# A decoder trunk on one core: where the tiles start in SBUF

## The chip, the cores and the metric

The kernel runs on one core of a Trainium2 chip. The metric is device time in microseconds (us), the median over several executions of one kernel; smaller is better. A profile is one execution, taken by the hardware profiler. PE (TensorE) multiplies matrices; a matmul has a stationary operand, which a weight load (PEld) puts into the array, and a moving operand that streams past it. DVE (VectorE) and ACT (ScalarE) do elementwise work, POOL (GpSimd) some of it, and SP (SyncE) issues all DMAs. All operands of PE come out of SBUF, which has 128 partitions; a tile of [128, 512] float32 takes 2,048 bytes in each partition, and its address is the byte at which it starts in every partition.

## What is computed

A sequence of 2,048 rows of width 1,024 goes through one retention layer and one sliding-window attention layer:

```
x = x + (rms(retention(q, k, v)) * silu(gate)) @ a_w_out      # 4 heads, chunks of 128
k, v = shared_kv(x)                                           # 2 key/value heads of 64
x = x + (swa(q, k, v, bias, sinks) * silu(gate)) @ b_w_out    # 16 heads, window of 128
```

with q, k, v and gate from an rms-normalised x times an input weight, a causal decay in the retention, and an attention over the block's own 128 keys and the 128 before, with a bias by distance and a sink in the softmax.

## The kernel before

**Precision.** Every large product is made of three matmuls in float32r: an operand `t` is split into `hi` (a rounded copy that ACT writes) and `lo = t - hi` (DVE, in the second layer partly POOL), and PE adds hi*hi, hi*lo and lo*hi into the same PSUM bank. `wload` (L104 to L124) does this with a weight tile: a DMA into a buffer with the tag "raw" (three buffers), the cast into "whi", the subtraction into "wlo". A matmul of this kind has a moving operand of [128, 512] and a stationary one of [128, 128]. In the rows a PE instruction is written as result<-moving,stationary.

**The retention layer (phase A).** 16 units, one for each of four row groups of 512 and four heads. `main` makes q and k (`project_qk`, L483 to L485, moving `xhi`/`xlo`, stationary `whi`/`wlo`), then v and gate: in the first four units with `proj` (L147 to L149, moving the weights, stationary x), in the other twelve with seven products of a Strassen scheme (`strassen`, L365 to L367), four of which take sums of x (`xhi_S`, `xlo_S`) as stationary operand. `ret` does the chunks of the retention: scores (L563), transposes of k (L583), the state's change (L604 to L606, moving `vhi`/`vlo`, stationary `khi`/`klo`), the output (L612 to L614, moving `Shi`/`Slo`, stationary `qhi`/`qlo`; L615 to L617, moving v, stationary `shi`/`slo`), transposes of the gated output (L640). `out_a` multiplies by the output weight (`pp_ao`, L143 to L145, moving `ohi_r`/`olo_r`, stationary `whi`/`wlo`).

**The attention layer (phase B).** 8 units: keys and values once for each group, q (L147 to L149), gates (L143 to L145, moving `xhi`), scores (L867), transposes of the probabilities (L888), the output (L904), the output projection (`pp_bo`, the same lines L143 to L145, moving `ohi_t`/`olo_t`).

**Order.** A scheduler interleaves the units; the program's order on each engine is fixed at build time.

**Where the tiles lie.** Pools lie one behind the other in SBUF in the order in which they are opened, and within a pool tiles lie in the order in which their tags first appear, each rounded up to 32 bytes: `const`, `xtp` (x hi and lo), `wp` (raw, whi, wlo), `small`, then the pools of phase A (`av` v, `ca` constants, `a1` most working tiles, `a2`, `ag` gate, `as` sums, `ax` the residual), which phase B's pools (`cb`, `b1`, `b2`) replace. Small tiles that come in between move all tiles behind them. In the built program, the starting bytes modulo 512 are:

| tiles | before | after the change |
|---|---|---|
| `ident`, `ident_r` | 128 | 0 |
| `ones` | 192 | 0 |
| `xhi`, `xlo`, raw, `whi`, `wlo` (all phases) | 320 | 0 |
| `vhi`, `vlo` | 192 | 0 |
| phase A: q, k, `ohi_r`, `olo_r`, `Shi`, `Slo`, `qhi`, `qlo`, `khi`, `klo`, `shi`, `slo`, gate, `xhi_S`, `xlo_S`, S, `x1` | 288 | 0 |
| phase B: `bias`, `kst`, `qs`, `qst`, `ohi_t`, `olo_t`, P, `pTs`, `vst`, `res`, gate | 320 | 0 |
| `rb` of `small` (read by DVE and POOL alone) | 320 | 128 |

A slice that PE reads starts a multiple of 512 bytes into its tile (`vst` and half of `qs` a multiple of 256), so the table holds for the operands too.

The functions that the change touches:

Of the kernel before, what the change touches and what calls it, by code (L numbers as in the profile page):

```python
# [12 lines left out]
F32 = mybir.dt.float32  # L13
F32R = mybir.dt.float32r
BF16 = mybir.dt.bfloat16
AF = mybir.ActivationFunctionType
# [3 lines left out]
P = 128  # L20
D = 1024
KT = D // P
T = 512
MT = T // P
RH = 4
DK = 256
DV = 512
HD = 64
QH = 16
KVH = 2  # L30
GQ = QH // KVH
EPS = 1e-6
NBUCK = 32
# [4 lines left out]
RAW = 3  # L38
# [20 lines left out]
def tile_yoco(ctx, tc, x, x_t, w_qk, w_vg, wo_a, w_kv, w_b, wo_b, ag, kvg, bg, kng, qng,  # L59
              relb, sinks, cos_t, sin_t, mask_t, vdec, epsd, onehot, out):  # L60
    nc = tc.nc
# [5 lines left out]
    const = ctx.enter_context(tc.tile_pool(name="const", bufs=1))  # L67
    xtp = ctx.enter_context(tc.tile_pool(name="xtp", bufs=1))
    wp = ctx.enter_context(tc.tile_pool(name="wp", bufs=3))
    small = ctx.enter_context(tc.tile_pool(name="small", bufs=4))  # L70
# [2 lines left out]
    xmid = [dram.tile([KT // 2, P, 2, T], F32, name=f"xmid{i}") for i in range(NG)]  # L73
    sqs = [dram.tile([P, T], F32, name=f"sqs{i}") for i in range(NG)]

    ident = const.tile([P, P], F32, name="ident")
    make_identity(nc, ident)
    ident_r = const.tile([P, P], F32R, name="ident_r")
    nc.vector.tensor_copy(ident_r, ident)
    neghalf = const.tile([P, GQ], F32, name="neghalf")  # L80
    nc.vector.memset(neghalf, -0.5)

    warm = const.tile([P, 1], F32, name="warm")
    nc.scalar.activation(warm, neghalf[:, :1], AF.Silu)

    ones = const.tile([P, P], F32, name="ones")
    nc.vector.memset(ones, 1.0)
    kvgs = const.tile([P, KT], F32, name="kvgs")
    bgs = const.tile([P, KT], F32, name="bgs")
    psum = {}  # L90

    def pbank(tag, name):
        return pp.tile([P, 512], F32, tag=tag, name=name)
# [104 lines left out]
    def bias_rows():  # L198


        oh = wp.tile([NBUCK + 1, 384], F32, tag="raw", bufs=RAW, name="oh")
        nc.sync.dma_start(oh, onehot)
        rb = const.tile([NBUCK + 1, QH], F32, name="rb")
        nc.vector.memset(rb, 1.0)
        nc.sync.dma_start(rb[:NBUCK, :], relb)
        bp = pbank("a", "biasp")
        nc.tensor.matmul(bp[:QH, :384], rb, oh, start=True, stop=True)
        bsb = wp.tile([QH, 384], F32, tag="raw", bufs=RAW, name="bsb")
        nc.vector.tensor_copy(bsb, bp[:QH, :384])
        nc.sync.dma_start(bd, bsb)  # L210
        yield
        for h in range(QH):
            nc.sync.dma_start(bdr[h], bd[h].partition_broadcast(P))
            yield
# [4 lines left out]
    def phase_a(pa):  # L219
        cst = pa["const"]  # L220
        p1, p2, vp, gp, xsp = pa["p1"], pa["p2"], pa["v"], pa["g"], pa["xs"]
        H = T // 2
        ags = cst.tile([P, KT], F32, name="ags")
        nc.sync.dma_start(ags, ag)
        mask = cst.tile([P, P], F32, name="mask")
        vd = cst.tile([P, RH], F32, name="vd")
        ep = cst.tile([P, RH], F32, name="ep")
        S_d = [dram.tile([P, 2, DV], F32, name=f"Sd{h}") for h in range(RH)]
        units = [(g, h) for g in range(NG) for h in range(RH)]
        nu = len(units)  # L230
# [310 lines left out]
        def ret(u):  # L541
            g, h = units[u]
            n = f"r{u}"
# [48 lines left out]
            for c in range(MT):  # L592
# [36 lines left out]
                        if c < MT - 1:  # L629
                            split_state(S32, d, parts)  # L630

                junk = small.tile([P, DV], BF16, tag="junk", bufs=1, name=f"jo_{n}_{c}")
                ss = small.tile([P, 1], F32, tag="ss1", name=f"sso_{n}_{c}")
                nc.scalar.activation(junk, op, AF.Square, accum_out=ss)  # L634
                r = rsqrt_mean(ss, DV, 1, f"o_{n}_{c}", eps=es[c])
# [67 lines left out]
        for _ in main(0):  # L703
            pass
        bias = bias_rows()
        for u in range(nu - 1):

            g, h = units[u + 1]
            if u + 1 in (1, 3, 4, 5):
                behind.append(stage_sums({1: 0, 3: 1, 4: 2, 5: 3}[u + 1]))  # L710
            if h == 2 and g + 1 < NG:
                behind.append(row_stats(g + 1))
                behind.append(stage_rows(g + 1))
            drive(tc, main(u + 1), ret(u), 2 if u + 1 < PLAIN else 3, 0)
            for _ in itertools.islice(bias, 2 if u >= RH else 0):
                pass
            if u < nu - 2:
                for _ in out_a(u):
                    pass
        pre = prep_b0()  # L720
        drive(tc, itertools.chain(out_a(nu - 2), itertools.islice(pre, 2)), ret(nu - 1), 1.5, 0)
        for _ in itertools.chain(out_a(nu - 1), pre):
            pass


    def phase_b(pb):
        cst = pb["const"]
        p1, p2 = pb["p1"], pb["p2"]
        gq = cst.tile([P, HD], F32, name="gq")
        gk = cst.tile([P, HD], F32, name="gk")  # L730
        nc.sync.dma_start(gq, qng.partition_broadcast(P))
# [1 line left out]
        nc.vector.scalar_tensor_tensor(gk, gk, HD ** -0.5, gq, op0=ALU.mult, op1=ALU.mult)  # L733
        snk = cst.tile([P, QH], F32, name="snk")
        nc.sync.dma_start(snk, sinks.partition_broadcast(P))
        nsnk = cst.tile([P, QH], F32, name="nsnk")
        nc.vector.tensor_scalar_mul(nsnk, snk, -1.0)
        bias = cst.tile([P, QH, 2 * P], F32, name="bias")
        nc.sync.dma_start(bias, bass.AP(tensor=bdr.tensor, offset=bdr.offset + P - 1,
                                        ap=[[383, P], [P * 384, QH], [1, 2 * P]]))  # L740

        units = [(g, kv) for g in range(NG) for kv in range(KVH)]
        nu = len(units)
        st = {"xt": first["xt"]}

        kst = cst.tile([P, KVH * 2, 2 * MT + 1, P], F32R, name="kst")

        def main(u):
            g, kv = units[u]
# [243 lines left out]
    with ExitStack() as es:  # L993
        mk = lambda name, bufs: es.enter_context(tc.tile_pool(name=name, bufs=bufs))
        psum["phase"] = "b"
        psum["pool"] = es.enter_context(tc.tile_pool(name="psb", bufs=1, space=bass.MemoryType.PSUM))
        phase_b(dict(const=mk("cb", 1), p1=mk("b1", 1), p2=mk("b2", 2)))
# [92 lines left out]
```

## Time and profile before

| | us |
|---|---|
| median of 3 runs (lowest, highest) | 2535.78 (2533.89, 2538.88) |
| the profiled execution: time | 2535.8 |
| the profiled execution: span from first to last instruction | 2534.0 |
| PE busy | 2469.2 (97%) |
| DVE busy | 1718.3 (68%) |
| ACT busy | 1128.5 (45%) |
| POOL busy | 476.7 (19%) |

How to read it: the busy time of PE counts a matmul from its start to its modelled end, and the matmuls overlap each other. A busy PE is therefore not a PE at its peak; how fast it really goes is read from the starts of matmuls that follow each other.

### The profile page before, as it was taken

The numbers are of one execution on the slowest core, as the hardware profiler recorded it, in microseconds if no ns is written. First come the engines' busy times: TensorE is split into PE (matmuls) and PEld (weight loads), VectorE is DVE, ScalarE is ACT, GpSimd is POOL, SyncE is SP. The second block draws the span as 40 slices with busy tenths as digits, with TensorE's granted clock in tenths as the row PEclk, the third lists the DMA queues.
The fourth block names the chain that finished last, engine by engine and source line by source line (L and its number), as shares of the span: only waits on it lengthen the run. The fifth ranks groups of instructions, "written<-read, shape, count | busy, mean of one in ns | idle before, by whom it ended". The sixth has DMA issues, their size and how long they took to land.

```text
span 2534.0 us, 32377 instructions
## 1 busy us (share of the span) xinstructions
PE 2469.2 (97%) x11816; PEld 1996.7 (79%) x11816; DVE 1718.3 (68%) x2953; ACT 1128.5 (45%) x2008; POOL 476.7 (19%) x393
## 2 busy tenths in 40 slices
PE   8999999999999999999999999999899999999998
PEld 6888787888888888888888888777677777777886
DVE  5546675785867667668666576677867677667766
ACT  4333233544435435436345344335544455444553
POOL 0000000110000020000020000042335444353360
PEclk9999999999999999999999999999899999999999
DMA  8434873576735445455354243364233342342432
GB/s 293 140 108 140 270 258 114 197 274 214 240 104 189 150 159 166 157 204 183 122 200 148 85 157 112 101 247 161 76 117 121 108 151 77 127 146 80 133 114 95
DMA packets 141035, 395.05 MB, mean 156 GB/s; under 512 B 16411, under 2 KB 28876, under 8 KB 140876
## 3 DMA queue, kind: packets, MB, share of 16 engines
q1 hardware_dynamic: 140876, 392.99, 46.7%
q8 instruction: 93, 1.52, 0.2%
q14 instruction: 66, 0.54, 0.1%
HBM read 321.60 MB, written 74.47 MB: 156 GB/s over the span
## 4 chain that ended last, share of the span: by engine, by line
PE 79%; DMA 9%; DVE 8%; ACT 2%; issue 1%; POOL 0%; SPq 0%; DVEq 0%; ACTq 0%
PE pp_ao L145 4%; PE pp_ao L143 4%; PE pp_ao L144 4%; PE o_t L904 2%; PE s_t L867 2%; PE pT_t L888 2%; PE pp_bo L143 1%; PE pp_bo L144 1%; PE pp_bo L145 1%; DMA res<-xmid 1%; DVE xlo_b L186 1%; PE o_r L613 1%; PE ot_r L640 1%; PE o_r L614 1%; PE o_r L612 1%
## 5 line engine op out<-in xcount | busy, mean ns | idle before, releaser
L143 PE MATMUL pp_ao<-ohi_r,whi_ao 128*128 128x512 f32 x512 | 201.6, 398 | 4.1 <-DVE x_r L676 2.1
L144 PE MATMUL pp_ao<-olo_r,whi_ao 128*128 128x512 f32 x512 | 203.7, 398 | 0.0
L101 POOL TENSOR_SCALAR r_o_r<-sso_r,ep 128x1 f32<-128x1 f32 x48 | 28.7, 597 | 920.8 <-ACT jo_r L634 920.8
L878 ACT ACTIVATE P_t<-P_t,nm_t 128x256 f32<-128x256 f32 (+1 forms) x256 | 127.7, 499 | 162.8 <-DVE nm_t L870 162.2
L145 PE MATMUL pp_ao<-ohi_r,wlo_ao 128*128 128x512 f32 x512 | 198.7, 398 | 0.1
L870 DVE CUSTOM_DVE_ANT_0 P_t<-s_t,bias,nsnk 128x256 f32<-128x256 f32 (+1 forms) x256 | 116.4, 470 | 38.7 <-PE s_t L867 37.8
L121 ACT CAST whi_ao<-raw_ao 128x1024 fp32r<-128x1024 f32 x64 | 67.1, 1048 | 155.5 <-issue 54.4
L123 DVE TENSOR_TENSOR wlo_ao<-raw_ao,whi_ao 128x1024 fp32r<-128x1024 f32 x64 | 78.2, 1223 | 83.9 <-ACT whi_ao L121 83.8
L700 ACT CAST Shi_r<-S 128x512 fp32r<-128x512 f32 x120 | 69.9, 617 | 114.8 <-PE o_r L614 89.8
L143 PEld LDWEIGHTS pp_ao<-ohi_r,whi_ao 128*128 128x128 f32 x512 | 96.1, 188 | 28.0 <-DVE x_r L676 2.5
L145 PEld LDWEIGHTS pp_ao<-ohi_r,wlo_ao 128*128 128x128 f32 x512 | 96.6, 189 | 24.6 <-DVE wlo_ao L123 1.2
L144 PEld LDWEIGHTS pp_ao<-olo_r,whi_ao 128*128 128x128 f32 x512 | 96.8, 189 | 23.2 <-issue 0.2
L867 PE MATMUL s_t<-kst,qst_b 128*128 128x256 f32 (+1 forms) x512 | 103.8, 300 | 9.2 <-DVE nm_t L870 9.0
L701 DVE TENSOR_TENSOR Slo_r<-S,Shi_r 128x512 fp32r<-128x512 f32 x120 | 85.3, 736 | 37.8 <-ACT Shi_r L700 37.8
L867 PEld LDWEIGHTS s_t<-kst,qst_b 128*128 128x128 f32 x512 | 84.9, 193 | 30.7 <-DVE nm_t L870 12.1
L627 DVE SCALAR_TENSOR_TENSOR S<-S,dl_r 128x512 f32<-128x512 f32 x112 | 74.6, 681 | 43.1 <-PE dl_r L606 42.9
L884 DVE TENSOR_SCALAR P_t<-P_t,den_t 128x256 f32<-128x256 f32 (+1 forms) x256 | 96.9, 441 | 1.8
L676 DVE TENSOR_TENSOR x_r<-x_r,pp_ao 128x512 f32<-128x512 f32 x128 | 84.4, 683 | 17.9 <-PE pp_ao L145 17.2
L143 PE MATMUL pp_bo<-ohi_t,whi_bo 128*128 128x512 f32 x224 | 89.4, 408 | 1.2 <-DVE gate_b L831 1.1
L144 PE MATMUL pp_bo<-olo_t,whi_bo 128*128 128x512 f32 x224 | 89.5, 399 | 0.0
L123 POOL TENSOR_TENSOR wlo_bo<-raw_bo,whi_bo 128x1024 fp32r<-128x1024 f32 x28 | 71.1, 2541 | 93.4 <-ACT whi_bo L121 87.0
L145 PE MATMUL pp_bo<-ohi_t,wlo_bo 128*128 128x512 f32 x224 | 88.0, 397 | 0.0
(1037 smaller groups left out, 7480.7 us busy)
## 6 DMA issues: line engine op xcount, KB each, us to landing
raw_ao<-in_wo_a SPq DMA_DIRECT2D x64, 512.0 KB, 3.6
b<-in_w_vg SPq DMA_DIRECT2D x64, 256.0 KB, 4.8
res<-xmid SPq DMA_DIRECT2D x56, 256.0 KB, 3.1
raw_bo<-in_wo_b SPq DMA_DIRECT2D x28, 512.0 KB, 3.6
x_r<-in_x_t SPq DMA_DIRECT2D x16, 512.0 KB, 5.7
xin<-in_x SPq DMA_DIRECT2D x16, 512.0 KB, 3.5
xmid<-x_r SPq DMA_DIRECT2D x16, 512.0 KB, 3.9
xraw_b<-xmid SPq DMA_DIRECT2D x16, 512.0 KB, 3.7
```

What stands on the lines that cost most here:

```text
L123: eng.tensor_tensor(lo, raw, hi.bitcast(F32), op=ALU.subtract)
L143: nc.tensor.matmul(o, hi[:, kk, sl], xh, start=st, stop=False)
L144: nc.tensor.matmul(o, hi[:, kk, sl], xl, start=False, stop=False)
L145: nc.tensor.matmul(o, lo[:, kk, sl], xh, start=False, stop=sp)
L627: nc.vector.scalar_tensor_tensor(S32[:, d, :], S32[:, d, :], gamC[h], dl[d], op0=ALU.mult, op1=ALU.add)
L676: nc.vector.tensor_tensor(t, t, ps, op=ALU.add)
L700: nc.scalar.copy(hi, src[:, d, :])
L701: nc.vector.tensor_tensor(lo, src[:, d, :], hi.bitcast(F32), op=ALU.subtract)
L867: nc.tensor.matmul(o, qst[m][:, h, :], kst[:, kv * 2 + hl, kb + b0 : kb + 2, :], start=hl == 0, stop=hl == 1)
L870: nc.vector.tensor_tensor_reduce(out=pt[:, j, :w], in0=o, in1=bias[:, kv * GQ + h, b0 * P :], scale=-1.0, scalar=nsv[:, h : h + 1], op0=AL ...
L878: nc.scalar.activation(pt[:, j, :w], pt[:, j, :w], AF.Exp, scale=-1.0, bias=nm[:, c : c + 1], accum_out=den[:, c : c + 1])
L884: nc.vector.tensor_scalar_mul(pt[:, j, :w], pt[:, j, :w], den[:, c : c + 1])
```

## The change

The contents of `const` are put in another order: the small tiles (`ags`, `vd`, `ep`, moved here out of phase A's pool, and `kvgs`, `bgs`, `rb`) come first, with `warm` widened to 32 columns as filling, and the 512-byte tiles behind them. The float32 identity is no longer a tile of its own: it is built in a raw buffer (`eye`), cast into `ident_r`, and `ident` becomes the same bytes read as float32. `junk` is widened by 64 columns so that `small` ends where the next pool starts at a multiple of 512. In phase B `bias` and `kst` come ahead of the small constants, and `nsnk` is widened as filling. The widened columns are not used by any instruction.

```diff
-    ident = const.tile([P, P], F32, name="ident")
-    make_identity(nc, ident)
-    ident_r = const.tile([P, P], F32R, name="ident_r")
-    nc.vector.tensor_copy(ident_r, ident)
+
     neghalf = const.tile([P, GQ], F32, name="neghalf")
     nc.vector.memset(neghalf, -0.5)
 
-    warm = const.tile([P, 1], F32, name="warm")
-    nc.scalar.activation(warm, neghalf[:, :1], AF.Silu)
-
+    warm = const.tile([P, 32], F32, name="warm")
+    nc.scalar.activation(warm[:, :1], neghalf[:, :1], AF.Silu)
+    ags = const.tile([P, KT], F32, name="ags")
+    kvgs = const.tile([P, KT], F32, name="kvgs")
+    bgs = const.tile([P, KT], F32, name="bgs")
+    vd = const.tile([P, RH], F32, name="vd")
+    ep = const.tile([P, RH], F32, name="ep")
+    relb_s = const.tile([NBUCK + 1, QH], F32, name="rb")
+
+    ident_r = const.tile([P, P], F32R, name="ident_r")
+    eye = wp.tile([P, P], F32, tag="raw", bufs=RAW, name="eye")
+    make_identity(nc, eye)
+    nc.vector.tensor_copy(ident_r, eye)
+    ident = ident_r.bitcast(F32)
     ones = const.tile([P, P], F32, name="ones")
     nc.vector.memset(ones, 1.0)
-    kvgs = const.tile([P, KT], F32, name="kvgs")
-    bgs = const.tile([P, KT], F32, name="bgs")
...
-        ags = cst.tile([P, KT], F32, name="ags")
         nc.sync.dma_start(ags, ag)
         mask = cst.tile([P, P], F32, name="mask")
-        vd = cst.tile([P, RH], F32, name="vd")
-        ep = cst.tile([P, RH], F32, name="ep")
...
-                junk = small.tile([P, DV], BF16, tag="junk", bufs=1, name=f"jo_{n}_{c}")
+                junk = small.tile([P, DV + 64], BF16, tag="junk", bufs=1, name=f"jo_{n}_{c}")[:, :DV]
...
+        bias = cst.tile([P, QH, 2 * P], F32, name="bias")
+
+        kst = cst.tile([P, KVH * 2, 2 * MT + 1, P], F32R, name="kst")
...
-        nsnk = cst.tile([P, QH], F32, name="nsnk")
+        nsnk = cst.tile([P, QH + P - HD // 2], F32, name="nsnk")[:, :QH]
...
-        bias = cst.tile([P, QH, 2 * P], F32, name="bias")
...
-        kst = cst.tile([P, KVH * 2, 2 * MT + 1, P], F32R, name="kst")
```

On every engine the instructions of the built program stand in the same order as before, with the same shapes. One DMA issue, that of the second weight tile, has one more wait, on DVE, since its buffer held `eye`.

## Rows read from the trace of the kernel before

**Rows 1.** The page: the span, the engines' busy time, the granted TensorE clock in 40 slices.

```profile
span 2534.0 us, 32377 instructions
PE 2469.2 (97%) x11816; PEld 1996.7 (79%) x11816; DVE 1718.3 (68%) x2953; ACT 1128.5 (45%) x2008; POOL 476.7 (19%) x393
PEclk9999999999999999999999999999899999999999
```

**Rows 2.** Busy time of each engine in three stretches: from:to, length, PE, PEld, DVE, ACT, POOL with the number of instructions; at the end the granted clock, the DMA engines' busy share and GB/s.

```profile
0.00:400.00 400.00, 382.32 (x1717) 312.16 (x1718) 241.31 (x330) 144.11 (x200) 23.11 (x46) 1.00 0.60 200
400.00:1640.00 1240.00, 1237.21 (x5603) 1007.85 (x5603) 843.01 (x1084) 556.04 (x798) 100.59 (x132) 1.00 0.50 164
1640.00:2534.00 894.00, 849.72 (x4500) 676.70 (x4497) 633.99 (x1539) 428.38 (x1012) 353.01 (x215) 0.97 0.37 124
```

**Rows 3.** The timeline of PE (start, length, engine, line, instruction), the first and the last matmul of an unbroken run of `pp_ao`; then the stretch between their starts, where the count of 70 includes one matmul that had begun before.

```profile
1649.53 0.39 PE L145 MATMUL pp_ao<-ohi_r,wlo_ao 128*128 128x512 f32 x1
...
1665.62 0.40 PE L145 MATMUL pp_ao<-ohi_r,wlo_ao 128*128 128x512 f32 x1
...
1649.53:1665.62 16.09, 16.09 (x70) 1.00 0.56 193
```

**Rows 4.** The same for a run of `pp_a8qk`, with 96 of which one had begun before.

```profile
823.13 0.39 PE L483 MATMUL pp_a8qk<-xhi_a,whi_a8qk 128*128 128x512 f32 x1
...
844.68 0.40 PE L485 MATMUL pp_a8qk<-xhi_a,wlo_a8qk 128*128 128x512 f32 x1
...
823.13:844.68 21.55, 21.55 (x96) 1.00 0.32 98
```

**Rows 5.** The timeline of PE, the first and the last of 24 matmuls of a Strassen product with a sum of x as stationary operand.

```profile
782.25 0.40 PE L365 MATMUL pp_a7va<-whi_a7v,xhi_S 128*128 128x512 f32 x1
...
787.62 0.40 PE L367 MATMUL pp_a7va<-whi_a7v,xlo_S 128*128 128x512 f32 x1
```

**Rows 6.** The timeline of PE in one chunk of the retention: the first of five matmuls of the state's change (L604 to L606), the first of the six of the output from the state (L612 to L614), and the first of the output from the chunk (L615).

```profile
125.42 0.39 PE L605 MATMUL dl_r<-vlo_a,khi_r 128*128 128x512 f32 x1
...
126.59 0.39 PE L612 MATMUL o_r<-Shi_r,qhi_r 128*128 128x512 f32 x1
...
127.95 0.40 PE L615 MATMUL o_r<-vhi_a,shi_r 128*128 128x512 f32 x1
```

**Rows 7.** The timeline of PE, a run of `pp_bo` behind a shorter matmul: its first, seventh, eighth and last (the twentieth).

```profile
1836.14 0.39 PE L145 MATMUL pp_bo<-ohi_t,wlo_bo 128*128 128x512 f32 x1
...
1837.53 0.39 PE L145 MATMUL pp_bo<-ohi_t,wlo_bo 128*128 128x512 f32 x1
1837.76 0.39 PE L143 MATMUL pp_bo<-ohi_t,whi_bo 128*128 128x512 f32 x1
...
1840.48 0.39 PE L143 MATMUL pp_bo<-ohi_t,whi_bo 128*128 128x512 f32 x1
```

**Rows 8.** Counts of matmuls: groups by line (busy us, mean ns of one, idle before); then, over the whole span, all that reads `xhi_S` and all that reads `xlo_S` (from:to, length, PE, PEld and so on with counts). L605 and L606 have the count of L604, L613 and L614 that of L612, L616 and L617 that of L615.

```profile
L143 PE MATMUL pp_ao<-ohi_r,whi_ao 128*128 128x512 f32 x512 | 201.6, 398 | 4.1 <-DVE x_r L676 2.1
L144 PE MATMUL pp_ao<-olo_r,whi_ao 128*128 128x512 f32 x512 | 203.7, 398 | 0.0
L145 PE MATMUL pp_ao<-ohi_r,wlo_ao 128*128 128x512 f32 x512 | 198.7, 398 | 0.1
L604 PE MATMUL dl_r<-vhi_a,khi_r 128*128 128x512 f32 x120 | 50.2, 418 | 0.0
L612 PE MATMUL o_r<-Shi_r,qhi_r 128*128 128x512 f32 x120 | 47.4, 395 | 0.0
L615 PE MATMUL o_r<-vhi_a,shi_r 128*128 128x512 f32 x64 | 25.3, 395 | 0.0
...
0.00:2534.00 2534.00, 250.57 (x768) 142.68 (x768) 15.87 (x13) 13.68 (x13) 0.99 0.47 156
...
0.00:2534.00 2534.00, 151.76 (x384) 72.03 (x384) 15.87 (x13) 0.99 0.47 156
```

**Rows 9.** Groups of DVE and ACT with the same shape (busy us, mean ns of one, idle before): subtraction and cast on tiles at 320, and on tiles at 288.

```profile
L123 DVE TENSOR_TENSOR wlo_ao<-raw_ao,whi_ao 128x1024 fp32r<-128x1024 f32 x64 | 78.2, 1223 | 83.9 <-ACT whi_ao L121 83.8
L575 DVE TENSOR_TENSOR qlo_r<-q_a,qhi_r 128x1024 fp32r<-128x1024 f32 x16 | 19.5, 1221 | 5.2 <-ACT qhi_r L574 4.8
L121 ACT CAST whi_ao<-raw_ao 128x1024 fp32r<-128x1024 f32 x64 | 67.1, 1048 | 155.5 <-issue 54.4 <-DMA raw_ao<-in_wo_a 23.2 <-PE pp_ao L144 21.3
L574 ACT CAST qhi_r<-q_a 128x1024 fp32r<-128x1024 f32 x16 | 16.8, 1052 | 12.7 <-PE o_r L613 12.6
```

**Rows 10.** The timeline of PE around small float32 matmuls: 16 scores and what follows them; and eight transposes of q in phase B.

```profile
139.81 1.95 PE L563 MATMUL sc_r<-q_a,k_a 128*128 128x128 f32 x16
141.59 0.38 PE L583 MATMUL kt_r<-ident,k_a 128*128 128x128 f32 x2
...
1730.91 0.84 PE L810 MATMUL qtp_b<-ident_r,qs_b 128*128 128x128 f32 x8 [0.15 <-ACT qst_b L814]
```

**Rows 11.** The timeline at the start: the cast of the identity, and the issues of the first two weight tiles.

```profile
1.32 0.23 DVE L79 CAST ident_r<-ident 128x128 fp32r<-128x128 f32 x1 [0.29 <-POOL ident masks.py:199]
1.64 0.91 SPq L113 DMA_DIRECT2D raw_a0qk<-in_w_qk  x2
```

**Rows 12.** The timeline of PE for two of its first matmuls, before the clock rises.

```profile
7.86 0.63 PE L484 MATMUL pp_a0qk<-xlo_a,whi_a0qk 128*128 128x512 f32 x1
8.29 0.63 PE L483 MATMUL pp_a0qk<-xhi_a,whi_a0qk 128*128 128x512 f32 x1
```

More of the change, by code (lines that the diff above doesn't have):

```diff
@@ L202, in bias_rows @@
         nc.sync.dma_start(oh, onehot)
-        rb = const.tile([NBUCK + 1, QH], F32, name="rb")
+        rb = relb_s
         nc.vector.memset(rb, 1.0)
```

## The prediction

> **What bounds the kernel now.** The page first: PE is busy for 2469.2 of 2534.0 us, no other engine over 68%, and its clock stands at the upper of its two levels (2.4 GHz) in nearly every slice [rows 1]. Then the busy time by stretches: from 400 to 1640 us, nearly all of phase A, PE stands idle for 2.8 of 1240 us, while DVE is busy for 843 and the DMA engines for half of the time; in the 400 us before it is idle for 17.7, and from 1640 us on, in phase B, for 44.3 of 894 [rows 2]. So in the middle stretch the time is the number of matmuls times their pace, and only what changes the pace of PE or the waits at both ends can move the total.
>
> The change adds no work and takes none away, so the pace is what has to be looked at. A matmul's length in the page (some 0.39 us) says nothing of it, because they overlap; I read the distance between the starts of matmuls that follow each other without a wait. All these are float32r with 512 columns, and they come in two paces. A run of `pp_ao` has 69 distances in 16.09 us, 233.2 ns each [rows 3]. A run of `pp_a8qk` has 95 in 21.55 us, 226.8 ns each [rows 4]. Why are they different? The first has its moving operand at 288 modulo 512 and its stationary one at 320; the second has both at 320. A Strassen product with the sums of x turns this round, moving operand at 320 and stationary one at 288, and again has 23 distances in 5.37 us, 233.5 ns [rows 5]. The state's change, moving at 192 and stationary at 288, has five in 1.17 us, 234 ns [rows 6]. That could still mean that 288 is a bad place to start. But the matmuls that follow there, with both operands at 288, have six in 1.36 us, 226.7 ns [rows 6]. And it isn't the line or the kind of work: `pp_bo` comes from the same three lines as `pp_ao`, only with both operands at 320, and settles at twelve distances in 2.72 us, 226.7 ns, after six that took 231.7 behind a shorter matmul [rows 7]. So every pair of operands with the same start modulo 512 runs at 226.7 to 226.8 ns, and every pair with different starts (by 32 or 96 bytes) at 233 to 234. What inside PE does this, no row tells; that it goes by the pair and not by the place is what the rows show.
>
> **The change part by part.**
>
> *Matmuls whose operands start differently.* Counted by group [rows 8]: `pp_ao` 3 x 512 = 1536; those with a sum of x 768 + 384 = 1152; the state's change 3 x 120 = 360; the output from the chunk 3 x 64 = 192. Together 3240. After the change both operands start at 0. At 233.3 - 226.8 = 6.5 ns for each this is 21.1 us.
>
> *Matmuls that start alike already.* The 360 of the output from the state [rows 8] and all others with 512 columns: nothing.
>
> *Settling.* Behind a change of pair or a shorter matmul some six distances cost 5 ns more [rows 7]. The changes of pair vanish, the shorter matmuls stay. A chunk has about three such changes, there are 64 chunks, so at most 64 x 3 x 6 x 5 ns = 5.8 us could go as well; on the other side, those of the 3240 that follow a short matmul won't reach 226.8. I take 0 and keep -2 to +6 us of gain.
>
> *Small matmuls.* The identity moves from 128 to 0, as do the tiles that it transposes. Counted from the loops these are 320 transposes in float32r (84 ns each, eight in 0.84 us less the last one's 0.25 [rows 10]) and 880 in float32. The scores, with both operands at 288, run at 1.78/16 = 111 ns [rows 10], but they are another kind. The nearest price is the 6.5 ns of the large ones, either way: 2 us for the 320, 5.7 us for the 880, of which more than half lie in phase B where PE has waits to lose. I take 0, and keep 3 us either way.
>
> *DVE, ACT, POOL.* The same subtraction takes 1223 ns on tiles at 320 and 1221 on tiles at 288; the cast 1048 and 1052 [rows 9]. No sign of an effect of the start: 0.
>
> *DMA.* All rows of a transfer now start at a multiple of 512 in SBUF. The trace has no transfer with such a start. The most that faster transfers could give is a part of PE's idle time at both ends, 17.7 + 44.3 = 62 us [rows 2], most of it waits on DVE and ACT; I take 0 and keep a tenth of it, 6 us, either way.
>
> *The start.* The second weight tile's load now waits for the cast of the identity, which ends at 1.55 us; that load is issued at about 2.1, the second half of the pair of issues that begins at 1.64 [rows 11]. Nothing, and what is queued behind it on SP isn't moved. If the cast were late, the first matmuls would be late by as much.
>
> *What of it reaches the end.* About four fifths of the 3240 lie in the middle stretch (all twelve Strassen units, twelve of sixteen output projections), where PE has no idle time to lose and nothing else is near its limit: 16.9 us, whole. Of the 4.2 us at the ends I count four fifths, since a faster PE there partly waits longer: 3.4. Sum 20.3 us. The profiled execution took 2535.8 us, which is the median (2535.78), so 2535.8 - 20.3 = **2515.5 us**, 0.8% faster.
>
> **The rivals.**
>
> *The starts don't matter.* The two paces would then come from something that goes with the tiles by chance, and nothing would change: 2535.8 us. Against it are three kinds of pairs that fit and the same lines at both paces [rows 3 to 7]; for it, that no row here changes a start alone. The Trainium skill ("TensorE: Matmul & The Clock Gate", step-by-step part of "What happens when you issue a matmul") says that PE has two independent read ports, so that loading the next weights takes no SBUF bandwidth from the running matmul. By that rule the pair could not matter and the time would stay 2535.8; the trace's 226.8 against 233.2 speaks against it. Chance 0.09.
>
> *The place counts as well as the pair.* 512 columns take 0.43 us at the lower clock, at the start of the trace [rows 12], that is twice 0.215, so some 12 ns of the 226.7 are more than the columns need. If a start at 0 took these away, about 9,000 matmuls (11,816 [rows 1] less the small ones) would gain 12 ns more, 108 us: about 2408 us, less whatever phase B then waits for. Against it: 288 and 320 differ in place by 32 bytes and give the same 226.7 [rows 6, 7]. Chance 0.06.
>
> *Slower: starts at 0 collide.* If operands that both begin at a multiple of 512 ran at the slow pace, the 5,700 that now run at 226.7 would cost 6.6 ns more, +38 us, with no gain on the 3240: 2573 us. It decides from the point where more of the 9,000 lose than gain. Against it: equal starts are the fast case at 288 and at 320 [rows 4, 6]. Chance 0.03.
>
> *The gain is given back.* DVE (68% of the middle stretch) or the loads become what PE waits for. Half of the gain would be left: 2525 us. Against it, 2.8 us of idle time in 1240 [rows 2]. Chance 0.04.
>
> **How the numbers follow.** The forecast has 0.78. Its own bounds: gain at most 21.1 + 6 + 3 + 6 = 36, at least 16.9 - 2 - 3 - 6 = 6; not all at once, so 2507 to 2524. To hold eight of ten cases the range takes in the half gain and reaches some way towards the place: **2502 to 2527**. Left out are no change, most of the place case, and slower, 0.17 together. A measurement of this kernel tells about 0.2%, 5 us, from no change (the three runs span 2533.9 to 2538.9): faster 0.78 + 0.06 + 0.04 = 0.88, same 0.09, slower 0.03.
>
> **What would show it right or wrong.** In the trace after, runs of `pp_ao` and of the Strassen products with sums should have distances of 226.7 ns, not 233; `pp_a8qk` and `pp_bo` should keep 226.7. Phase B should be as long as before and phase A about 20 us shorter. If `pp_ao` still shows 233, the pair isn't the cause; if all show under 220, the place counts too; if the distances fall but the span doesn't, look at PE's idle time between 400 and 1640 us. Subtractions and casts of 128x1024 should stay at 1.22 and 1.05 us; should they move, the DVE and ACT step was wrong.

## The result and the profile after

The changed kernel takes 2520.24 us, median of six executions (2513.12 to 2522.16), against 2536.16 for six of the kernel before (2532.87 to 2541.76): a ratio of 0.993 with a 95% interval of 0.9912 to 0.9947. Two later comparisons with the same kernel, told below, gave 2519.13 against 2538.16 (0.9918, 0.9901 to 0.9935) and 2518.11 against 2539.45 (0.992, 0.9903 to 0.9937). In the last of these one of six executions of the changed kernel took 8630.76 us; it is left out, and no run shows why. The differences are 15.9, 19.0 and 21.3 us, 18.8 on the mean. I had forecast 20.3 less and 2515.5, with a range of 2502 to 2527.

The profiled execution of the changed kernel is the fastest of its six, 2513.12 us. The page, lines that answer to [rows 1]:

```profile
span 2511.3 us, 32377 instructions
PE 2446.6 (97%) x11816; PEld 1995.4 (79%) x11816; DVE 1714.5 (68%) x2953; ACT 1128.1 (45%) x2008; POOL 477.2 (19%) x393
PEclk9999999999999999999999999999899999999999
```

PE is busy for 22.6 us less, with the same 11,816 matmuls; DVE, ACT and POOL do what they did. The three stretches of [rows 2], now of the changed kernel (from:to, length, PE, PEld, DVE, ACT, POOL with counts; granted clock, DMA share, GB/s):

```profile
0.00:400.00 400.00, 380.51 (x1697) 311.91 (x1698) 237.02 (x324) 141.62 (x196) 23.29 (x46) 0.98 0.60 199
400.00:1640.00 1240.00, 1237.20 (x5687) 1023.87 (x5686) 852.02 (x1104) 562.00 (x807) 106.79 (x136) 1.00 0.51 165
1640.00:2511.30 871.30, 828.92 (x4436) 659.57 (x4434) 625.50 (x1527) 424.48 (x1007) 347.15 (x212) 0.98 0.38 127
```

In the middle stretch PE has no more idle time than before (2.8 us), but does 5,687 matmuls in it instead of 5,603. In the first 400 us it does fewer, 1,697 instead of 1,717, at a granted clock of 0.98 instead of 1.00. That was a surprise, and some of the experiments go after it.

The timeline of PE for the runs of [rows 3] (`pp_ao`), [rows 4] (`pp_a8qk`), [rows 5] (Strassen) and [rows 7] (`pp_bo`): the first and last matmul of each, for the first two also the stretch with its count, which includes one matmul that had begun before:

```profile
1634.20 0.40 PE L151 MATMUL pp_ao<-ohi_r,wlo_ao 128*128 128x512 f32 x1
...
1649.88 0.39 PE L151 MATMUL pp_ao<-ohi_r,wlo_ao 128*128 128x512 f32 x1
...
1634.20:1649.87 15.67, 15.67 (x70) 1.00 0.58 195
...
820.69 0.40 PE L486 MATMUL pp_a8qk<-xhi_a,whi_a8qk 128*128 128x512 f32 x1
...
842.25 0.39 PE L488 MATMUL pp_a8qk<-xhi_a,wlo_a8qk 128*128 128x512 f32 x1
...
820.69:842.24 21.55, 21.55 (x96) 1.00 0.31 98
...
780.86 0.39 PE L368 MATMUL pp_a7va<-whi_a7v,xhi_S 128*128 128x512 f32 x1
...
786.07 0.39 PE L370 MATMUL pp_a7va<-whi_a7v,xlo_S 128*128 128x512 f32 x1
...
1819.60 0.40 PE L151 MATMUL pp_bo<-ohi_t,wlo_bo 128*128 128x512 f32 x1
...
1823.92 0.39 PE L149 MATMUL pp_bo<-ohi_t,whi_bo 128*128 128x512 f32 x1
```

The run of `pp_ao` has its 69 distances in 15.68 us, 227.2 ns each, where it took 16.09. The Strassen run has 23 in 5.21 us, 226.7 ns, where it took 5.37. `pp_a8qk` takes 21.55 us for 95 as before, and `pp_bo` 4.32 for 19 (4.34 before). And the chunk of [rows 6], the second matmul of the state's change (L608), the first of the output from the state, the first of the output from the chunk:

```profile
126.29 0.40 PE L608 MATMUL dl_r<-vlo_a,khi_r 128*128 128x512 f32 x1
...
127.44 0.40 PE L615 MATMUL o_r<-Shi_r,qhi_r 128*128 128x512 f32 x1
...
128.83 0.39 PE L618 MATMUL o_r<-vhi_a,shi_r 128*128 128x512 f32 x1
```

Five distances in 1.15 us and six in 1.39: 230 and 232 ns. In this one chunk the output from the state is slower than it was [rows 6]: transposes stand right ahead of the state's change, and behind them the pace takes until the output from the chunk to settle. One chunk is no measure. Over the whole trace the mean distance between neighbours of one kind is given below, worked out from the starts of all matmuls. The number is that of the matmuls; the mean is over the distances below 260 ns, which are fewer (207 for the state's change and 97 for the output from the chunk, over 1,000 for the first two kinds):

| kind | number | before | after |
|---|---|---|---|
| `pp_ao` | 1536 | 233.3 | 227.0 |
| sums of x | 1152 | 233.3 | 227.3 |
| state's change | 360 | 232.3 | 228.6 |
| output from the chunk | 192 | 233.2 | 226.6 |
| output from the state (alike before, too) | 360 | 230.7 | 227.6 |

The engines beside PE, groups that answer to [rows 9], and the start, rows that answer to [rows 11]:

```profile
L129 DVE TENSOR_TENSOR wlo_ao<-raw_ao,whi_ao 128x1024 fp32r<-128x1024 f32 x64 | 78.1, 1223 | 81.7 <-ACT whi_ao L127 80.3 <-PE dl_r L609 1.3
L127 ACT CAST whi_ao<-raw_ao 128x1024 fp32r<-128x1024 f32 x64 | 67.2, 1050 | 153.1 <-issue 47.5 <-PE pp_ao L150 25.8 <-DMA raw_ao<-in_wo_a 24.2
...
1.32 0.23 DVE L92 CAST ident_r<-eye 128x128 fp32r<-128x128 f32 x1 [0.29 <-POOL eye masks.py:199]
...
1.64 0.91 SPq L119 DMA_DIRECT2D raw_a0qk<-in_w_qk  x2
```

Subtraction and cast last what they lasted, and the pair of weight loads is issued at 1.64 us, as before.

### The profile page after: what moved, and what is told of

Same layout as the page of the kernel before. It is cut to its first block, busy times and chain, and to the rows that moved or that the text cites. A ratio compares the mean times of both kernels' runs of the same rounds, so it can differ in the third digit from the quotient of the medians.

```text
span 2511.3 us, 32377 instructions
## 1 busy us (share of the span) xinstructions
PE 2446.6 (97%) x11816; PEld 1995.4 (79%) x11816; DVE 1714.5 (68%) x2953; ACT 1128.1 (45%) x2008; POOL 477.2 (19%) x393
## 4 chain that ended last, share of the span: by engine, by line
PE 81%; DMA 8%; DVE 7%; ACT 2%; issue 1%; POOL 0%; SPq 0%; DVEq 0%; ACTq 0%
PE pp_ao L151 4%; PE pp_ao L149 4%; PE pp_ao L150 4%; PE o_t L907 2%; PE s_t L870 2%; PE pT_t L891 2%; PE pp_bo L149 1%; PE pp_bo L150 1%; PE pp_bo L151 1%; DMA res<-xmid 1%; PE ot_r L643 1%; PE dl_r L607 1%; PE o_r L615 1%; PE dl_r L608 1%; PE o_r L617 1%
## 5 line engine op out<-in xcount | busy, mean ns | idle before, releaser
L127 ACT CAST whi_ao<-raw_ao 128x1024 fp32r<-128x1024 f32 x64 | 67.2, 1050 | 153.1 <-issue 47.5
L129 DVE TENSOR_TENSOR wlo_ao<-raw_ao,whi_ao 128x1024 fp32r<-128x1024 f32 x64 | 78.1, 1223 | 81.7 <-ACT whi_ao L127 80.3
```

Source lines behind the costliest of these rows:

```text
L129: eng.tensor_tensor(lo, raw, hi.bitcast(F32), op=ALU.subtract)
```

## The experiments

Two things had to be settled: whether it is the pair that sets the pace, and where the rest of the difference between the two profiles belongs, since the start was slower and the end faster than forecast. The comparison throughout is between kernels whose 3240 pairs are alike and kernels where they aren't.

### One mask wider, in the kernel before

```diff
-        mask = cst.tile([P, P], F32, name="mask")
+        mask = cst.tile([P, P + 8], F32, name="mask")[:, :P]
```

> The kernel before with one edit: the causal mask of phase A is 8 float32 columns wider, so that all of phase A's tiles behind it (q, k, the split output, the split state, the sums of x) move from 288 to 320 modulo 512, where x and the weights already lie. v stays at 192. Nothing begins at a multiple of 512. Theory of the pair (the pace goes by whether both operands start alike): the output projection's 1536 and the 1152 matmuls with a sum of x fall from 233.3 to 226.8 ns, 2688 x 6.5 ns = 17.5 us; the state's change and the output from the chunk (552, v at 192 against 320) stay at 233 to 234, or show what a distance of 128 bytes does. Time 2518 to 2520 us. Theory of the place (a multiple of 512 is what helps): no pace changes, 2536 us.

Measured: 2523.58 us against 2538.16, ratio 0.993 (0.9912 to 0.9948). The run of `pp_ao` in this kernel:

```profile
1635.95 0.39 PE L145 MATMUL pp_ao<-ohi_r,wlo_ao 128*128 128x512 f32 x1
...
1651.62 0.39 PE L145 MATMUL pp_ao<-ohi_r,wlo_ao 128*128 128x512 f32 x1
```

15.67 us for the 69 distances: 227.1 ns, with operands at 320 and no large operand at a multiple of 512. Eight unused columns bring 14.6 us of the 17.5 expected, and the time lies 3.6 us above the range given. The state's change, now 128 bytes apart, stays at 232.1 ns. The output from the chunk, 128 apart too, has a median of 234 ns but a mean of 229.9, as its distances are some 224 or some 234. The theory of the place falls for the pace.

### All tiles 32 bytes on, in the changed kernel

```diff
-    warm = const.tile([P, 32], F32, name="warm")
+    warm = const.tile([P, 40], F32, name="warm")
```

> The changed kernel with `warm` 40 columns wide instead of 32: every tile of 2 KB and more moves from 0 to 32 modulo 512, all of them together, so every pair of operands still starts alike. Theory of the pair: all paces 226.7 to 226.9 ns as in the changed kernel, time 2513 to 2524 us, no different from it. Theory of the place: the paces of the output projection and the Strassen sums are back at 233 ns, the time at 2536 us or above; and if a start at 32 hurts the transfers or DVE, their durations are longer than those of the changed kernel.

Measured: 2522.16 us, ratio to the kernel before 0.9927 (0.9907 to 0.9947), within the scatter of the changed kernel. `pp_ao`:

```profile
1640.55 0.40 PE L151 MATMUL pp_ao<-ohi_r,wlo_ao 128*128 128x512 f32 x1
...
1656.22 0.39 PE L151 MATMUL pp_ao<-ohi_r,wlo_ao 128*128 128x512 f32 x1
```

Again 15.67 us. A multiple of 512 is worth nothing by itself to PE. For the other engines and the transfers the durations say the same: subtraction and cast of 128x1024 take 1223 and 1050 ns, as in the changed kernel, and the loads of `raw_ao` land 3.7 us after their issue (median), against 3.6 in the kernel before and in the changed kernel. The median is 3.0 us above the 2519.13 of the changed kernel in the same comparison, which is less than such comparisons tell.

### The pairs apart again, in the changed kernel

```diff
-        mask = cst.tile([P, P], F32, name="mask")
+        mask = cst.tile([P, P + 8], F32, name="mask")[:, :P]
```

> The changed kernel with the mask of phase A 8 columns wider: phase A's working tiles behind it move to 32 modulo 512, while x, the weights and v stay at 0. The 3240 matmuls that had unlike operands in the kernel before are unlike again, by 32 bytes; all else of the change stays. Theory of the pair: output projection, Strassen sums, state's change and output from the chunk at 233 to 234 ns, the gain of the change gone: 2520 + 21 = 2541 us, 2536 to 2545. Theory that another part of the change made the gain (order of the small tiles, the shared identity, phase B's order): time stays at 2520 us.

Measured: 2539.29 us, ratio to the kernel before 1.0001 (0.9989 to 1.0012). `pp_ao` and the Strassen run of unit 7:

```profile
1656.82 0.39 PE L151 MATMUL pp_ao<-ohi_r,wlo_ao 128*128 128x512 f32 x1
...
1672.91 0.40 PE L151 MATMUL pp_ao<-ohi_r,wlo_ao 128*128 128x512 f32 x1
...
787.49 0.40 PE L368 MATMUL pp_a7va<-whi_a7v,xhi_S 128*128 128x512 f32 x1
...
792.86 0.40 PE L370 MATMUL pp_a7va<-whi_a7v,xlo_S 128*128 128x512 f32 x1
```

16.09 and 5.37 us, to the hundredth what [rows 3, 5] show. The same edit that gained 14.6 us in the kernel before costs the changed kernel 20.2 us (2539.29 against 2519.13 in the same comparison), its whole gain. So the rest of the change, the new order of `const`, the shared identity, phase B's order, is worth nothing within some 3 us.

### The changed kernel once more

No edit.

> The changed kernel again, unaltered, for what differs from one execution to the next. In its first profile the matmul that stands at 400 us in the kernel before came 4.7 us later, and phase B was 7.4 us shorter. If these belong to the change, this profile shows them again: the same matmul 4 to 5 us later, phase B 6 to 8 us shorter, time about 2513 us. If they come from the execution (how long the first transfers take, how often PE falls to its lower level), they differ: the start anywhere from -2 to +6 us, phase B from -8 to 0, while the stretch from 400 to 1640 us is again 19 to 21 us shorter. Time 2513 to 2524 us.

Measured: 2519.13 us. The matmul of 400 us came 5.3 us later than in the first profile of the kernel before, so the start's loss was there again; phase B was only 2.2 us shorter, not 7.4, and the stretch from 400 to 1640 us 17.3 us shorter, less than the 19 expected (19.9 in the first profile of the changed kernel). That left open whether the start's loss belongs to the change. Four profiles with the new order of `const` had it by then, one of the kernel before and one with the wider mask had not.

### All alike at 416, with the old front of const

Against the kernel before; the three tiles leave phase A's pool.

```diff
     bgs = const.tile([P, KT], F32, name="bgs")
+    ags = const.tile([P, KT], F32, name="ags")
+    vd = const.tile([P, RH], F32, name="vd")
+    ep = const.tile([P, RH], F32, name="ep")
...
-                junk = small.tile([P, DV], BF16, tag="junk", bufs=1, name=f"jo_{n}_{c}")
+                junk = small.tile([P, DV + 64], BF16, tag="junk", bufs=1, name=f"jo_{n}_{c}")[:, :DV]
...
-        nsnk = cst.tile([P, QH], F32, name="nsnk")
+        nsnk = cst.tile([P, QH + 96], F32, name="nsnk")[:, :QH]
```

> The kernel before with three small edits: `ags`, `vd` and `ep` (96 bytes) stand at the end of `const` instead of in phase A's pool, `junk` is 64 columns wider, `nsnk` 96 columns wider. By that x, the weights, v, all working tiles of both phases lie at 416 modulo 512, so every pair of large operands starts alike, but nothing lies at a multiple of 512; the identity keeps its own tile at 128, and the front of `const` and the first loads are those of the kernel before. Theory of the pair: all 3240 matmuls at 226.7 to 227.5 ns, time as for the changed kernel, 2516 to 2522 us. On the first 400 us: if their loss of 4 to 7 us (four profiles with the changed order of `const`, against none in the kernel with the wider mask) comes with the changed order, it is absent here, the matmul of 400 us stands at -2 to 0 against before, and the time is 3 to 5 us below that of the changed kernel; if it comes with the execution or with PE being faster than the loads, it is here too and the times are the same within 2 us.

Measured: 2519.06 us, ratio 0.9919 (0.9904 to 0.9933), and the changed kernel beside it 2518.11: the same. `pp_ao` at 227 ns:

```profile
1634.89 0.40 PE L148 MATMUL pp_ao<-ohi_r,wlo_ao 128*128 128x512 f32 x1
...
1650.54 0.39 PE L148 MATMUL pp_ao<-ohi_r,wlo_ao 128*128 128x512 f32 x1
```

Its matmul of 400 us came 1.7 us later than in the first profile of the kernel before: between the two expectations. With its identity at 128 and the tiles at 416, transposes keep their median of 108 to 109 ns.

### The identity built in another buffer

```diff
-    eye = wp.tile([P, P], F32, tag="raw", bufs=RAW, name="eye")
+    eye = wp.tile([P, P], F32, tag="whi", name="eye")
```

> The changed kernel, only that the float32 identity is built in a buffer of the tag whi instead of a raw buffer: the second weight tile's load has no wait on DVE any more, and the raw buffers are handed out in the same turn as in the kernel before. All starts as in the changed kernel. If the loss of the first 400 us comes from the identity in a raw buffer, it is gone here (matmul of 400 us at -2 to +1 us against before, time 3 to 5 us below that of the changed kernel); if not, it is +4 to +7 us again and the time is that of the changed kernel, 2516 to 2522 us. The paces stay at 226.7 to 227.5 ns.

Measured: 2518.88 us, the same as the changed kernel beside it, and the matmul of 400 us 3.5 us late. The wait of the second load on DVE shows no cost.

### The changed kernel beside these two

> The changed kernel unaltered, beside the two others: a third profile of its start and the time that they are compared with. If the start's loss belongs to it, its matmul of 400 us is again 4 to 7 us later than in the kernel before; time 2516 to 2522 us, the stretch from 400 to 1640 us 19 to 21 us shorter.

Measured: 2518.11 us, the median of five; the matmul of 400 us came 3.7 us late, a little less than the 4 to 7 expected, and the stretch from there to 1640 us was 18.6 us shorter, a little less than the 19 to 21 expected.

### The kernel before once more

> The kernel before unaltered, a second profile of it: if the start of a profile varies by itself, its matmul of 400 us stands some us away from the first profile's; if the loss belongs to the change, within 2 us of it. The stretch from 400 to 1640 us takes the same 1240 us within 1 us, and phase B shows how much its length varies without a change (the first profile: ten stretches at the lower clock after 1640 us).

Measured: 2541.26 us for this one execution, and the start's loss is here without any change: the matmul of 400 us came 5.3 us later than in the first profile. The stretch up to 1640 us took 1241.8 us (1240.0 in the first), more apart than the 1 us expected; phase B took 1.7 us less. The first matmul of unit 0's gate, behind its wait, and two of those that follow:

```profile
59.45 0.50 PE L147 MATMUL pp_a0g<-whi_a0g,xhi_a 128*128 128x512 f32 x1 [2.62 <-DVE vlo_a L411]
...
60.40 0.63 PE L147 MATMUL pp_a0g<-whi_a0g,xhi_a 128*128 128x512 f32 x1
60.83 0.63 PE L148 MATMUL pp_a0g<-wlo_a0g,xhi_a 128*128 128x512 f32 x1
```

The wait is 2.62 us here and 1.54 in the first profile of the same kernel; DVE stands there behind operations on weights that are still being loaded. Behind the longer wait the matmuls are 0.43 us apart, the lower of the clock's levels: from 59.0 to 63.5 us the granted clock is 0.62 here and 1.00 in the first profile. So the first 400 us differ by 5 us from one execution to the next, and the first profile of the kernel before was a lucky one. What had looked like a cost of the change was at least in the main the profile it was compared with.

### How far apart

The changed kernel with the mask 16, 32 and 64 columns wider, that is with pairs 64, 128 and 256 bytes apart:

```diff
-        mask = cst.tile([P, P], F32, name="mask")
+        mask = cst.tile([P, P + 16], F32, name="mask")[:, :P]
```

> The changed kernel with the mask of phase A 16 columns wider: phase A's working tiles lie at 64, x, weights and v at 0, so the 3240 pairs are 64 bytes apart. If any difference costs the same: output projection and Strassen sums at 233.3 ns, 2519 + 19 = 2538 us. If only some bits of the start count (32 does): 226.8 ns and 2519 us.

> The same with 32 columns, the 3240 pairs 128 bytes apart. If any difference costs the same: 233.3 ns, 2538 us (the output from the chunk at 128 bytes apart in the kernel with the wider mask had a median of 234 ns). If a start counts only modulo 128 or less: 226.8 ns, 2519 us.

> The same with 64 columns, the 3240 pairs 256 bytes apart. If starts count modulo 512: 233.3 ns, 2538 us. If they count modulo 256 or less: 226.8 ns, 2519 us.

Measured, in this order: 2534.71 us (ratio 0.9983, 0.9971 to 0.9996), 2535.43 (0.9987, 0.9973 to 1.0002), 2519.41 (0.9917, 0.9894 to 0.9941), against 2538.91. The run of `pp_ao` at 64, at 128 and at 256, and the Strassen run at 64:

```profile
1654.67 0.40 PE L151 MATMUL pp_ao<-ohi_r,wlo_ao 128*128 128x512 f32 x1
...
1670.48 0.39 PE L151 MATMUL pp_ao<-ohi_r,wlo_ao 128*128 128x512 f32 x1
```

```profile
1651.95 0.39 PE L151 MATMUL pp_ao<-ohi_r,wlo_ao 128*128 128x512 f32 x1
...
1667.98 0.39 PE L151 MATMUL pp_ao<-ohi_r,wlo_ao 128*128 128x512 f32 x1
```

```profile
1639.16 0.40 PE L151 MATMUL pp_ao<-ohi_r,wlo_ao 128*128 128x512 f32 x1
...
1654.83 0.39 PE L151 MATMUL pp_ao<-ohi_r,wlo_ao 128*128 128x512 f32 x1
```

```profile
788.12 0.39 PE L368 MATMUL pp_a7va<-whi_a7v,xhi_S 128*128 128x512 f32 x1
...
793.49 0.40 PE L370 MATMUL pp_a7va<-whi_a7v,xlo_S 128*128 128x512 f32 x1
```

256 bytes apart is as good as alike: 15.67 us, 227.1 ns. 128 apart costs 16.03 us, 232.3 ns. 64 apart it depends on which operand is ahead: `pp_ao`, moving operand at 64 and stationary one at 0, takes 15.81 us, 229.1 ns (mean of all its runs 229.8), while the Strassen product, the other way round, takes 5.37, 233.5 ns. So the starts count modulo 256, not modulo 512, as far as the one difference of 256 that was tried shows, and the price is not quite one number: the output from the chunk, 128 apart, has a mean of 230.8 ns here.

### The output projection of phase B apart

```diff
-        nsnk = cst.tile([P, QH + P - HD // 2], F32, name="nsnk")[:, :QH]
+        nsnk = cst.tile([P, QH + P - HD // 2 + 8], F32, name="nsnk")[:, :QH]
```

> The changed kernel with `nsnk` 8 columns wider: phase B's tiles behind it (`qs`, `qst`, `ohi_t`, `olo_t`, P, `pTs`, `vst`) lie at 32, while x, the weights, `kst` and the identity stay at 0. Theory of the pair: the runs of `pp_bo` go from 227.1 to 233 ns, 672 x 6.5 = 4.4 us more in phase B if all of it reaches the end; nothing else of the large matmuls changes. For the small ones it is the test of my zero: scores with 256 columns, transposes of the probabilities and of q, and the last projection now have operands that start 32 bytes apart; zero means that their distances stay as in the changed kernel, the other bound is 6.5 ns each.

Measured: 2521.89 us, one execution, too few for a difference of 4 us. The run of [rows 7]:

```profile
1824.72 0.40 PE L151 MATMUL pp_bo<-ohi_t,wlo_bo 128*128 128x512 f32 x1
...
1829.15 0.39 PE L149 MATMUL pp_bo<-ohi_t,whi_bo 128*128 128x512 f32 x1
```

4.43 us for 19 distances, 233.2 ns, where the changed kernel has 4.32. Over all distances of `pp_bo` the mean goes from 229.8 to 233.2 ns: 3.4 ns each and not the 6.5 expected, 2.3 us for the 672, since the mean of `pp_bo`, unlike its settled pace, stood above 227 already. The small matmuls, medians of the distance between neighbours of one kind, changed kernel and this one: transposes of the probabilities 109 and 109 ns, transposes of q 82 and 82, scores with 256 columns 118 and 120, the last projection with 256 columns 120 and 117. Two kinds keep their pace, one loses 2 ns and one gains 3: nothing like the 6.5 of the large ones.

## Why the prediction was right, and where it was off

**The whole, by stretches.** For all profiles, the start of the first matmul of unit 4's q and k (`pp_a4qk`), from there to the first of phase B's (`pp_b0kv`), and from there to the last matmul's start, in us:

| kernel | pairs | to unit 4 | unit 4 to phase B | phase B |
|---|---|---|---|---|
| before, first profile | 32, 96 apart | 408.4 | 1261.0 | 860.6 |
| before, second | 32, 96 apart | 413.8 | 1264.5 | 857.3 |
| changed, mask +8 | 32 apart | 414.1 | 1262.7 | 853.2 |
| changed, mask +16 | 64 apart | 415.6 | 1259.1 | 859.3 |
| changed, mask +32 | 128 apart | 412.7 | 1259.2 | 855.6 |
| before, mask +8 | v 128 apart | 407.5 | 1248.5 | 855.9 |
| changed, three profiles | alike | 412.9, 413.5, 411.9 | 1241.3, 1245.5, 1244.3 | 853.2, 857.0, 853.7 |
| changed, all at 32 | alike | 415.1 | 1245.4 | 859.4 |
| changed, other buffer | alike | 411.7 | 1244.6 | 856.6 |
| all at 416 | alike | 409.9 | 1244.9 | 857.4 |
| changed, mask +64 | 256 apart | 411.0 | 1248.1 | 853.3 |
| changed, `nsnk` +8 | alike, `pp_bo` 32 apart | 412.8 | 1245.1 | 858.3 |

The two marks, in the first profiles of before and of after, and in the kernel with pairs 32 apart:

```profile
408.45 0.39 PE L483 MATMUL pp_a4qk<-xhi_a,whi_a4qk 128*128 128x512 f32 x1
...
1669.48 0.58 PE L147 MATMUL pp_b0kv<-whi_b0kv,xhi_b 128*128 128x256 f32 x1 [3.46 <-ACT whi_b0kv L121]
```

```profile
412.87 0.39 PE L486 MATMUL pp_a4qk<-xhi_a,whi_a4qk 128*128 128x512 f32 x1
...
1654.17 0.58 PE L153 MATMUL pp_b0kv<-whi_b0kv,xhi_b 128*128 128x256 f32 x1 [3.91 <-ACT whi_b0kv L127]
```

```profile
414.05 0.40 PE L486 MATMUL pp_a4qk<-xhi_a,whi_a4qk 128*128 128x512 f32 x1
...
1676.79 0.58 PE L153 MATMUL pp_b0kv<-whi_b0kv,xhi_b 128*128 128x256 f32 x1 [3.48 <-ACT whi_b0kv L127]
```

The middle column alone separates the kernels. It is 1262.7 on the mean of the first three rows and 1244.3 on the mean of the six profiles that are alike in all large operands: 18.4 us. Profiles of one kernel differ in it by 3 to 4 us, so the 18.4 is good to some 2 us. Both outer columns scatter by 7 to 8 us, and kernels with pairs alike and pairs apart lie in each other's range. That the first profile of after had a phase B 7.4 us shorter than the first of before (7.3 between these marks), where I had said "as long as before", is such scatter.

**Matmuls whose operands start differently: right, as a mechanism, and in size for the long runs.** The distances fell from 233.2 or 233.3 ns to between 226.6 and 227.3 for three of the four kinds; the state's change, whose short runs stand behind transposes, fell by 3.7 instead of 6.5. "That it goes by the pair and not by the place is what the rows show" is now shown by edits of the start alone, in both directions. The rule "modulo 512" was too narrow: the rows of before held no pair 256 apart.

**Settling, right within its bounds, but not nothing.** I had taken 0. Behind a run whose operands start apart, a run whose operands start alike is slow at first: in the kernel before, the first five distances of the q and k runs that follow `pp_ao` in the middle stretch have a mean of 231.0 ns, in the changed kernel 226.7. So matmuls that start alike before and after gained, too. Between the first two marks the sums of the distances (mean of the first three rows less mean of the six) fell by 1.1 us for the output from the state, by 1.2 for q and k and by 1.5 for v and gate without the sums of x, 3.8 us together. Against it, the four kinds of the 3240 brought less than 6.5 ns each: 8.0, 6.7, 1.0 and 1.1 us (`pp_ao`, sums of x, state's change, output from the chunk), 16.7 us together.

**What reaches the end: the term that was mis-sized, twice.** "About four fifths of the 3240 lie in the middle stretch", 16.9 us. Counted in the trace, 2775 start between 400 and 1640 us (86%), 369 ahead and 96 behind; between unit 4's first matmul and phase B it is 2835, with 405 ahead and none behind. By the forecast's own price 2835 x 6.5 = 18.4 us, and 18.4 us were measured. That they agree to the tenth is luck: the 18.4 measured are the 16.7 of the four kinds and the 3.8 of the others, less 2.1 us for more waits and slow distances (all above 380 ns). For the ends I had counted 3.4 us. Between these marks only the 405 ahead could give anything, 2.6 us, and their stretch shows 412.9 on the mean of the first five rows and 412.5 with the six alike: 0.4, within a scatter of 8. PE has waits there (17.7 us without work in [rows 2], 19.5 in the changed kernel), and I take it that what a faster PE wins it waits longer; the scatter is too large to show it. Too little in the middle and too much at the ends nearly made up for each other: 20.3 forecast, 18.8 measured in the medians.

**The baseline.** 4.7 us lay between forecast and median; 1.5 are the gain. The other 3.2 I put down to the starting point, the median of three, to which the difference was applied: "The profiled execution took 2535.8 us, which is the median". Over later comparisons the kernel before had 2538.2 to 2539.5. None of this is clear of the noise: a gain of 20.3 us lies within the interval of each of the three comparisons.

**The rest at nothing: right.** DVE and ACT [rows 9] kept their durations. All starts at 0, at 32 or at 416 gave the same time within 3 us, and the loads of `raw_ao` landed after the same 3.6 to 3.7 us, which leaves nothing measurable for the transfers. The start's wait on the identity's cast shows no cost beside the kernel without it. The small matmuls kept their pace (medians of float32 transposes 109 ns before, 108 and 109 after; scores of phase A 112 and 112).

**The rivals.** "The starts don't matter" is refuted by the kernel with pairs 32 apart: the changed kernel but for eight unused columns, and 20.2 us slower. The Trainium skill ("TensorE: Matmul & The Clock Gate", step-by-step part of "What happens when you issue a matmul") gives PE two independent read ports, so that a weight load takes no SBUF read bandwidth from the running matmul; by that rule, as I read it, these two kernels would take the same time, and the measurement (2539.29 against 2519.13 us) decides against that for this stream of float32r matmuls with a new stationary operand each. "The place counts as well" and "starts at 0 collide" both fall with 227 ns at 0, 32, 320 and 416. "The gain is given back" happened in small. Shortly ahead of unit 8's q and k, PE waits for the cast of `whi_ao`, whose weights are still being loaded. With pairs apart (the first five rows) it waits 0 to 0.7 us there; in the first profile of the changed kernel not at all; in the other kernels whose 3240 pairs are alike 0.5 to 1.4 us; and in the two kernels mask +8 before and mask +64 after 2.0 us. There the clock falls behind the wait, which it doesn't behind a wait of 1.4 us in the second profile of the changed kernel. The wait and the lower clock behind it are most of why these two stand at 1248 in the middle column, some 4 us above the kernels that are alike; in mask +8 before, the pairs with v have a part in it. The two waits, mask +8 before and changed kernel, and the stretch with the granted clock (0.53) in the first:

```profile
790.55 0.53 PE L143 MATMUL pp_ao<-ohi_r,whi_ao 128*128 128x512 f32 x1 [2.00 <-ACT whi_ao L121]
...
791.10:794.50 3.40, 3.40 (x9) 2.34 (x9) 3.40 (x5) 3.04 (x6) 0.81 (x2) 0.53 0.44 151
```

```profile
794.57 0.50 PE L149 MATMUL pp_ao<-ohi_r,whi_ao 128*128 128x512 f32 x1 [1.38 <-ACT whi_ao L127]
```

**What stays open.** Which load meets which stream: in a long run every stationary operand lies at the same start, so that the matmul's own and the next one's, loaded while it streams, can't be told apart. Nor is it shown why a pair 64 bytes apart costs less one way round than the other, or why the output from the chunk, 128 apart, has distances of some 224 beside some 234 ns. Starts between these steps were not tried, nor other types than float32r for the large matmuls.

## What to carry to other kernels

When float32r matmuls of 512 columns with a new stationary operand each run at two paces, compare the starts of their two operands modulo 256 first: here padding some tile ahead by a few unused columns was the whole remedy, and gathering everything at multiples of 512 is not needed. Multiply the price by the count in the stretch where the engine has no idle time, from the trace and not by eye; where the engine waits, write the gain off. And before a difference of some us between two profiles is explained, look at a second profile of the same kernel: here the stretches with waits differed by 5 to 8 us on their own.

## What the runs showed of the hardware

- Float32r matmuls with 512 columns and a new stationary operand each follow each other every 226.7 ns, once settled, when both operands start alike modulo 256 (0 or 256 bytes apart; at 0, 32, 288, 320 and 416 alike). In long runs it is 232 to 233.5 ns when the starts are 32 or 128 bytes apart; 64 apart it is 229.1 to 229.8 ns with the moving operand ahead and 233.0 to 233.5 with the stationary one ahead. In short runs 96 apart it is 232.3 and 233.2 ns on the mean, and 128 apart 229.9 to 233.4.
- A run whose operands start alike keeps some of the slower pace at its beginning when it follows a run whose operands start apart: 231.0 ns on the mean of the first five distances of q and k behind `pp_ao`, against 226.7 when all start alike.
- Matmuls of 128 or 256 columns showed no such step: with starts alike and 32 apart 109 and 109, 82 and 82 ns (128 columns), 118 and 120, 120 and 117 ns (256 columns).
- The same matmul of the same kernel came at 400.1 and at 405.4 us in two executions; there, a wait of 2.62 us instead of 1.54 was followed by a stretch at the lower clock, 0.43 us from matmul to matmul.
